# Expert weights through nine buffers and three split pieces, with regrouped gathers, in a two-layer hybrid block

## The chip, the cores and the metric

The kernel runs on one core of a Trainium2 chip. The metric is the device time of one execution in microseconds (us); lower is better. Engines are called PE (matmul; PEld is its weight load), DVE (vector), ACT (scalar), POOL (GpSimd) and SP (the engine whose queue issues the DMAs).

## The reference, cut to what matters

Two layers, each a token mixer and then a channel mixer. The second layer's channel mixer is the stage that the change touches: 256 tokens, width 1024, eight experts of hidden width 2816, two chosen for each token, everything in float32.

```python
def swiglu(x, w1, w3, w2):
    return (jax.nn.silu(x @ w1) * (x @ w3)) @ w2

def moe_swiglu(x, router, w1, w3, w2):
    logits = (x @ router).astype(jnp.float32)
    top_v, top_i = lax.top_k(logits, TOP_K)
    wts = jax.nn.softmax(top_v, axis=-1)
    gate = jnp.sum(jax.nn.one_hot(top_i, N_EXPERTS, dtype=jnp.float32) * wts[..., None], axis=-2)
    out = jnp.zeros(x.shape[:-1] + (w2.shape[-1],), x.dtype)
    for e in range(N_EXPERTS):
        out = out + gate[..., e:e + 1].astype(x.dtype) * swiglu(x, w1[e], w3[e], w2[e])
    return out
```

After it, `x = x + mod[5] * rms_norm(f, g_ffn_post[l])`: the residual x is needed again at the very end.

## The kernel before, in words

Everything up to the second layer's output projection is outside the change. At its end the router chooses experts, and `moe` starts. Each expert's three weight matrices (w1, w3, w2) are read once, each as 11 **chunks** of 1 MB (128 partitions by 2048 floats), so an expert is 33 chunks and the stage 264. A framework orders each engine's instructions ahead of time by priority and program order and adds the semaphores; a tile of a pool waits until the tile that held its slot before is released.

The experts run in the order q = 0 to 7 with the kinds `KINDS = "LSSLSSLS"`; which expert comes at which place is worked out on the device (`in_order`), so that the fuller ones come where room is larger. A **large** expert (`large`, room for 128 tokens) cuts each chunk into two **pieces** of 1024 columns. `split` (L366 to L368) rounds a piece on ACT into `hi`, and DVE subtracts it into `lo`; PE then multiplies hi by the tokens' hi, lo by hi, and hi by the tokens' lo: three matmuls where one would do at full precision of the operands (L1275 to L1277 for w1 and w3, L1366 to L1368 for w2). A chunk's buffer is free when DVE has made its second lo; a piece is free when PE has read it. A **small** expert (`small`, room for 64 tokens) multiplies the chunk itself, two column halves side by side (L1294, L1415); its buffer is free when PE has read it. Between the passes a large expert has `outer` (Silu on ACT, L1334) and `inner` (a product on DVE, four transposes on PE, a split, L1343 to L1349); the first two `inner` come before w2, four more within it.

`raw` (L1145) names the buffer of each chunk in the order of use: two tiles that are idle at the start (`sa0` and `kept`), then five `early` ones, each used once, and in between and ever after a ring. Before, that ring has six: three slots of the tag "raw" (the same that the earlier stages use) and three of the 13 slots of 8 KB a partition of the pool tag "S8". `piece_e` turns through five piece pairs: three of the tags "hi" and "lo", two more in S8. The 13 S8 slots in the experts' stage hold the normalized tokens (2), the ring (3), the tokens of large experts (`xes`, 2), the hidden values (`parts_u`, 3), the extra pieces (2) and the output sum (1). The trace calls S8 tiles "big".

`dispatch(qs, ...)` gathers the tokens of the experts qs with 32 matmuls (L1042) and scales them on ACT (L1204), and splits them for a large expert. `experts` runs it for `GROUPS[1:]` during the w3 pass of the experts `AT_GROUP`. The residual sits in an S8 tile until it is copied to `kept` (four ACT copies, L1439), and `kept` is itself the buffer of the second chunk.

SP's queue holds the weight loads in order; a load waits there for its buffer, and everything behind it waits too.

Of the kernel before, what the change touches and what calls it, by code (L numbers as in the profile page):

```python
# [10 lines left out]
R32 = mybir.dt.float32r  # L11
# [6 lines left out]
P = 128  # L18
D = 1024
KD = 8  # L20
# [8 lines left out]
N_AAC = 2  # L29
RATES = (0.661, 1.71, 1.045, 0.616, 1.995, 1.467, 0.55)  # L30
N_RAW = 3
N_RAW2, N_PC2 = 3, 2
N_PC = 3
N_EARLY = 5
LEAD = 3
# [11 lines left out]
AT_BACK, AT_NEXT = 2, 1  # L47
KINDS = "LSSLSSLS"
RANKS = (0, 1, 5, 2, 3, 6, 4)
GROUPS = ((0,), (1, 2, 3), (4, 5, 6), (7,))  # L50
AT_GROUP = (0, 2, 5)
ROOM = {"L": 128, "S": 64}
START = (0, 1, 2, 3, 'x', 'ctx')
# [3 lines left out]
def hybrid_kernel(ctx, tc, x, c, ctx_in, c_ctx, ada_w, ada_b, g_mix_pre, g_mix_post, g_ffn_pre, g_ffn_post,  # L57
# [4 lines left out]
    V, S, G, PE, SY = nc.vector, nc.scalar, nc.gpsimd, nc.tensor, nc.sync  # L62
# [12 lines left out]
    def nm(s):  # L75
        n_made[0] += 1
        return f"{s}{n_made[0]}"
# [7 lines left out]
    def sm(n, dt=F32):  # L85
        return st_.tile([P, n], dt, tag="sm", bufs=24, name=nm("sml"))
# [10 lines left out]
    def hot():  # L97
        return tc.high_priority(offset=PRI)
# [277 lines left out]
    def piece(shape):  # L376
        hi = st_.tile([P] + shape, R32, tag="hi", bufs=N_PC, name=nm("hi"))
        lo = st_.tile([P] + shape, R32, tag="lo", bufs=N_PC, name=nm("lo"))
        return hi, lo
# [686 lines left out]
    def moe(l, xt, route):  # L1066
# [12 lines left out]
        def weights():  # L1079
# [16 lines left out]
            PE.matmul(pr, ones, sel[:, 1], start=False, stop=True)  # L1096
            V.tensor_copy(cnt, pr)

        def in_order():

            key, rank = sm(NE), sm(N1)
            V.scalar_tensor_tensor(key, cnt, float(NE), ie, op0=OP.mult, op1=OP.add)
            square = lambda: s2([N1, N1])
            rows = lambda v: v.unsqueeze(1).to_broadcast([P, N1, N1])
            cols = lambda v: v.unsqueeze(2).to_broadcast([P, N1, N1])
            less, here = square(), square()
            V.tensor_tensor(less, rows(key[:, 1:]), cols(key[:, 1:]), op=OP.is_lt)
            V.tensor_reduce(rank, less, AX.X, OP.add)
            V.tensor_tensor(here, rows(rank), cols(rankq), op=OP.is_equal)
            yield  # L1110
            order, lens = sm(NE), sm(NE)
            todo = [(order, ie), (lens, cnt)] + [(to[:, t], of[:, t]) for to, of in ((slots, route.slot), (gates, gate)) for t in range(2)]
            for to, of in todo:
                picked = square()
                V.tensor_tensor(picked, here, rows(of[:, 1:]), op=OP.mult)
                V.tensor_reduce(to[:, 1:], picked, AX.X, OP.add)
                V.tensor_copy(to[:, 0:1], of[:, 0:1])
                yield
            V.tensor_copy(orderi, order)
            for q in range(NE):  # L1120
                if ROOM[KINDS[q]] < P:
                    V.tensor_scalar(lens[:, q:q + 1], lens[:, q:q + 1], float(P - ROOM[KINDS[q]]), None, op0=OP.add)
            V.reduce_max(most, lens, AX.X)
            V.tensor_copy(mosti, most)
# [13 lines left out]
                return self.tiles[(self.used - 1) % self.n]  # L1138
        sa0 = mo.tile([P, 1536 + 22 * 64], F32, name="sa")
        kept = mo.tile([P, 2 * D], F32, name="kept")  # L1140
        raws, xes, parts_u, pieces = Ring(N_RAW2, [2048]), Ring(2, [2, KD, P], R32), Ring(3, [2, 8, P], R32), Ring(N_PC2, [2, 1024], R32)
        ridx, early = [0], []
        inif = [False]

# [83 lines left out]
        def in_turn(*gens):  # L1228
            for g in gens:
                yield from g  # L1230
# [6 lines left out]
                        return  # L1237
                n = n and n - 1

        pidx = [0]  # L1240

        def piece_e():
            pidx[0] += 1
            if pidx[0] % (N_PC + N_PC2) < N_PC or inif[0]:
                return piece([1024])
            both = pieces()
            return both[:, 0], both[:, 1]

        def banks(ps, n, before):
            while len(ps) <= n:  # L1250
                if before:
# [3 lines left out]
        def flat_pass(wf, xe, aside=None, at=0, before=None):  # L1255

            ps = []
            for ch in range(11):
                if ch >= at:
                    run(aside, 1)  # L1260
                rw = raw(wf[:, ch * 2048:(ch + 1) * 2048])
                for hf in range(2):
                    with hot():
                        hi, lo = piece_e()
                        split(hi, lo, rw[:, hf * 1024:(hf + 1) * 1024])
                    f = ch * 2048 + hf * 1024
                    end = f + 1024
                    f_ = f
                    while f_ < end:
                        k, col = divmod(f_, FF)  # L1270
                        w = min(512 - col % 512, FF - col, end - f_)
                        banks(ps, col // 512, before)
                        o = ps[col // 512][:, col % 512:col % 512 + w]
                        hs, ls_ = hi[:, f_ - f:f_ - f + w], lo[:, f_ - f:f_ - f + w]
                        PE.matmul(o, xe[:, 0, k], hs, start=(k == 0), stop=False, skip_group_check=True)  # L1275
                        PE.matmul(o, xe[:, 0, k], ls_, start=False, stop=False, skip_group_check=True)
                        PE.matmul(o, xe[:, 1, k], hs, start=False, stop=(k == KD - 1), skip_group_check=True)  # L1277
                        f_ += w
            return ps
# [42 lines left out]
        def large(q, xe, behind, ahead):  # L1322

            pa = flat_pass(weight(moe_w1, q, "(p k) n -> p (k n)", k=KD), xe, behind, AT_BACK)
            run(behind)

            def cols(j):
                w = min(512, FF - 512 * j)
                return sa0[:, 512 * j:512 * j + w], w

            def outer(j):
                d, w = cols(j)
                with hot():
                    S.activation(d, pa[j][:, :w], AF.Silu)  # L1334
            yield
            pb = flat_pass(weight(moe_w3, q, "(p k) n -> p (k n)", k=KD), xe, ahead, AT_NEXT, outer)
            run(ahead)
            us = [parts_u() for _ in range(3)]

            def inner(j):  # L1340
                d, w = cols(j)
                with hot():
                    V.tensor_tensor(d, d, pb[j][:, :w], op=OP.mult)  # L1343
                    pt = tp()
                    dv = d.rearrange("s (a p r) -> s a r p", p=P, r=2)
                    for n in range(w // P):
                        PE.transpose(pt[:, n * P:(n + 1) * P], dv[:, n // 2, n % 2], ident)
                    o = slice(4 * j % 8, 4 * j % 8 + w // P)
                    split(us[j // 2][:, 0, o], us[j // 2][:, 1, o], pt[:, :w].rearrange("p (n s) -> p n s", s=P))  # L1349
            for j in range(U0):  # L1350
                inner(j)
            w2v = weight(moe_w2, q, "(a p r) n -> a p (r n)", p=P, r=2)
            py = [mm(), mx()]
            for a_ in range(11):
                rw = raw(w2v[a_])
                if a_ >= U1 and (a_ - U1) % 2 == 0 and U0 + (a_ - U1) // 2 < 6:
                    inner(U0 + (a_ - U1) // 2)
                for r in range(2):
                    with hot():
                        hi, lo = piece_e()  # L1360
                        split(hi, lo, rw[:, r * 1024:(r + 1) * 1024])
                    k = 2 * a_ + r
                    uh, ul = us[k // 8][:, 0, k % 8], us[k // 8][:, 1, k % 8]
                    for n in range(2):
                        cs = slice(n * 512, (n + 1) * 512)
                        PE.matmul(py[n], uh, hi[:, cs], start=(k == 0), stop=False)  # L1366
                        PE.matmul(py[n], uh, lo[:, cs], start=False, stop=False)
                        PE.matmul(py[n], ul, hi[:, cs], start=False, stop=(k == 21))  # L1368
            yield py
# [48 lines left out]
        def experts(base, fresh):  # L1418

            xs, backs, behind, group = [], [], None, []  # L1420
            before = dict(zip(AT_GROUP, GROUPS[1:])) if fresh else {q - 1: (q,) for q in range(1, NE)}
            if fresh:
                xs.append(xes())
                with tc.high_priority(offset=2 * PRI):
                    route.second_half(xs[0])
                weights()
                behind = in_order()
            else:
                run(dispatch((0,), base, xs))
            for q in range(NE):  # L1430
# [2 lines left out]
                    ahead.append(dispatch(before[q], base, xs))  # L1433
                do = (large if base or KINDS[q] == "L" else small)(q, xs.pop(0), behind, in_turn(*ahead))
                next(do)
                if fresh and q == 0:
                    for t in range(2):
                        for c in range(2):
                            S.copy(kept[:, 1024 * t + 512 * c:1024 * t + 512 * c + 512], xt[:, t, 512 * c:512 * c + 512])  # L1439
                if fresh and q == NE - 2:  # L1440
                    row = mo.tile([P, 2, 512], F32, name="row")
                    rows.extend([row[:, c] for c in range(2)])
# [9 lines left out]
                behind = None  # L1452
                if q % 2 or q == NE - 2:
                    behind = send_back(group, fresh and q == 1)
# [163 lines left out]
```

## Time and profile before

| | |
|---|---|
| median of 3 runs | 2069.02 us (2067.56 to 2077.01) |
| profiled execution | 2069.72 us, of which the span of the trace is 2068.0 us |
| PE busy | 1955.6 us (95% of the span) |
| DVE busy | 1306.7 us (63%) |
| ACT busy | 807.5 us (39%) |
| experts' stage | from about 1338 us to the end |
| DMA | 456.55 MB, mean 221 GB/s |

Busy time is a sum over the whole span and says little of one stage. The idle time of an engine is listed with what ended it. Matmuls overlap: a matmul of 512 columns is shown as 0.39 us long while the next starts 0.23 us after it, so distances between starts are the measure of PE's pace.

### The profile page before, as it was taken

Reading aid. Unit: us, or ns where it says so; the run is one execution under the profiler, and the core shown is the slowest. Engines: PE = TensorE matmul, PEld = TensorE weight load, DVE = VectorE, ACT = ScalarE, POOL = GpSimd, SP = SyncE. Lnnn points to the kernel's source line nnn. Section 1 sums busy time; section 2 is a strip of 40 time slices with the busy share of each in tenths; the row PEclk is TensorE's granted clock in tenths of the full one; section 3 lists DMA queues with packets and bytes.
Section 4 is the critical chain, followed back from the end, with each engine's and each line's share of the span. In section 5 each row is a group of like instructions: output and inputs, shape, how many; then the busy total and the mean of one; then the engine's idle time right before and its main releaser. Section 6 shows DMA issues by size and latency. Waiting matters only on the chain. (4 is left out here: it accounts for less than half of the span.)

```text
span 2068.0 us, 26249 instructions
## 1 busy us (share of the span) xinstructions
PE 1955.6 (95%) x9975; PEld 1423.8 (69%) x9975; DVE 1306.7 (63%) x2246; ACT 807.5 (39%) x1310; POOL 111.0 (5%) x183
## 2 busy tenths in 40 slices
PE   7999999989989999999999999999998999999996
PEld 3878777767878887887787889787332873437842
DVE  4896776689889869638976776787010870007812
ACT  3333334534352222226533475586020750006700
POOL 1000210030010000001002111000000000000000
PEclk9999999999999999999899999899999999999998
DMA  8324322335536567525333236569999989999996
GB/s 292 90 84 120 85 84 72 112 102 164 183 102 199 173 206 237 182 82 163 107 104 110 83 109 217 224 234 343 420 406 420 410 327 380 405 421 393 354 371 258
DMA packets 168197, 456.55 MB, mean 221 GB/s; under 512 B 11840, under 2 KB 84992, under 8 KB 134272
## 3 DMA queue, kind: packets, MB, share of 16 engines
q1 hardware_dynamic: 168064, 454.80, 60.3%
q8 instruction: 80, 1.31, 0.3%
q14 instruction: 53, 0.43, 0.1%
HBM read 450.05 MB, written 1.05 MB: 218 GB/s over the span
## 5 line engine op out<-in xcount | busy, mean ns | idle before, releaser
L385 PE MATMUL mm<-big,hi 128*128 128x512 f32 (+2 forms) x1328 | 481.4, 363 | 5.3 <-DVE mid L769 3.1
L386 PE MATMUL mm<-big,hi 128*128 128x512 f32 (+2 forms) x1328 | 476.3, 359 | 0.3 <-DVE sml L134 0.2
L387 PE MATMUL mm<-big,lo 128*128 128x512 f32 (+2 forms) x1328 | 475.7, 358 | 0.1
L367 ACT CAST hi<-raw 128x1024 fp32r<-128x1024 f32 (+1 forms) x276 | 286.3, 1046 | 471.1 <-PE mm L386 283.9
L368 DVE TENSOR_TENSOR lo<-raw,hi 128x1024 fp32r<-128x1024 f32 (+1 forms) x276 | 336.5, 1227 | 159.2 <-ACT hi L367 148.0
L385 PEld LDWEIGHTS mm<-big,hi 128*128 128x128 f32 (+1 forms) x1328 | 253.2, 191 | 56.6 <-issue 7.2
L386 PEld LDWEIGHTS mm<-big,hi 128*128 128x128 f32 (+1 forms) x1328 | 253.0, 191 | 42.6 <-issue 3.5
L387 PEld LDWEIGHTS mm<-big,lo 128*128 128x128 f32 (+1 forms) x1328 | 253.0, 190 | 40.1 <-issue 0.5
L276 DVE SCALAR_TENSOR_TENSOR aac<-raw,csil,aac 128x512 f32<-128x512 f32 x224 | 163.3, 765 | 2.9 <-DMA raw<-in_ada_w_dram 1.8
L1397 DVE TENSOR_TENSOR sa<-sa,mm 128x512 f32<-128x512 f32 x5 | 3.4, 689 | 218.7 <-PE mm L1294 218.7
L519 DVE SCALAR_TENSOR_TENSOR big<-ci,cdw,big 128x512 f32<-128x512 f32 (+1 forms) x240 | 132.9, 611 | 0.8
L1294 PE MATMUL mx<-big,mid 128*64 128x512 f32 (+1 forms) x358 | 99.3, 528 | 8.0 <-DMA big<-in_moe_w_dram 7.3
L1294 PE MATMUL mx<-raw,mid 128*64 128x512 f32 (+1 forms) x342 | 93.7, 518 | 6.4 <-DMA raw<-in_moe_w_dram 5.9
L1450 DVE SCALAR_TENSOR_TENSOR mid<-mm,sml,mid 128x512 fp32r<-128x512 f32 x8 | 6.0, 751 | 128.1 <-ACT mid L1449 128.1
L368 DVE TENSOR_TENSOR lo<-big,hi 128x1024 fp32r<-128x1024 f32 x61 | 72.9, 1221 | 9.2 <-ACT hi L367 8.4
L440 PE MATMUL mm<-hi,big 128*128 128x512 f32 x186 | 73.5, 395 | 0.0
L441 PE MATMUL mx<-lo,big 128*128 128x512 f32 x186 | 73.3, 394 | 0.0
L440 PE MATMUL mx<-hi,big 128*128 128x512 f32 x186 | 73.3, 394 | 0.0
L441 PE MATMUL mm<-lo,big 128*128 128x512 f32 x186 | 73.3, 394 | 0.0
L442 PE MATMUL mm<-hi,big 128*128 128x512 f32 x186 | 73.1, 393 | 0.0
L442 PE MATMUL mx<-hi,big 128*128 128x512 f32 x186 | 73.0, 393 | 0.0
L1294 PEld LDWEIGHTS mx<-big,mid 128*64 128x64 f32 x358 | 33.8, 140 | 53.9 <-issue 29.2
(414 smaller groups left out, 3310.4 us busy)
## 6 DMA issues: line engine op xcount, KB each, us to landing
big<-in_moe_w_dram SPq DMA_DIRECT2D x134, 1024.0 KB, 8.4
raw<-in_moe_w_dram SPq DMA_DIRECT2D x128, 1024.0 KB, 9.4
raw<-in_w_in_dram SPq DMA_DIRECT2D x56, 1024.0 KB, 5.3
raw<-in_ada_w_dram SPq DMA_DIRECT2D x41, 1024.0 KB, 5.1
raw<-in_ffn_w_dram SPq DMA_DIRECT2D x34, 1024.0 KB, 5.8
raw<-in_w_out_dram SPq DMA_DIRECT2D x8, 1024.0 KB, 5.1
big<-in_ada_w_dram SPq DMA_DIRECT2D x7, 1024.0 KB, 14.4
raw<-in_gla_proj_dram SPq DMA_DIRECT2D x4, 1024.0 KB
```

What stands on the lines that cost most here:

```text
L276: V.scalar_tensor_tensor(a, aw[:, k - 4 * r], col, a, op0=OP.mult, op1=OP.add)
L367: S.copy(hi, src)
L368: (eng or V).tensor_tensor(lo, src, hi, op=OP.subtract)
L385: PE.matmul(ps, hi[:, k, m0:m1], xh, start=(k == 0), stop=False)
L386: PE.matmul(ps, hi[:, k, m0:m1], xl, start=False, stop=False)
L387: PE.matmul(ps, lo[:, k, m0:m1], xh, start=False, stop=(k == kn - 1))
L440: PE.matmul(pss[t], a, hi[:, kk - k], start=(kk == 0), stop=False)
L441: PE.matmul(pss[t], a, lo[:, kk - k], start=False, stop=False)
L442: PE.matmul(pss[t], b, hi[:, kk - k], start=False, stop=(kk == kn - 1))
L519: V.scalar_tensor_tensor(acc, win, tap, acc, op0=OP.mult, op1=OP.add)
L1294: PE.matmul(ps[col // 1024][half:half + 64, col % 512:col % 512 + w], xe[:, k], rw[:, f_:f_ + w], start=(k == 0), stop=(k == KD - 1), skip ...
L1450: V.scalar_tensor_tensor(y[1], p_, back[1], y[0], op0=OP.mult, op1=OP.subtract)
```

## The change

The ring of chunk buffers grows from six to nine: `N_RAW2` is 6 instead of 3, so six S8 slots and the three "raw" slots. The extra pieces in S8 go (`piece_e` is removed; every piece is one of the three hi/lo pairs), and there is one `xes` tile instead of two. For that, the gathers are grouped otherwise: experts 1 and 2 during expert 0, then 3, 4, 5 during expert 2, then 6 and 7 during expert 5. The four copies of the residual to `kept` move from behind the w1 and w3 passes of expert 0 in the program into its w1 pass (`put_by`, two copies at each of two steps, ahead of `in_order`).

```diff
-N_RAW2, N_PC2 = 3, 2
+N_RAW2 = 6
...
-GROUPS = ((0,), (1, 2, 3), (4, 5, 6), (7,))
+GROUPS = ((0,), (1, 2), (3, 4, 5), (6, 7))
...
+        def put_by():
+
+            for t in range(2):
+                for c in range(2):
+                    S.copy(kept[:, 1024 * t + 512 * c:1024 * t + 512 * c + 512], xt[:, t, 512 * c:512 * c + 512])
+                yield
+
...
-        raws, xes, parts_u, pieces = Ring(N_RAW2, [2048]), Ring(2, [2, KD, P], R32), Ring(3, [2, 8, P], R32), Ring(N_PC2, [2, 1024], R32)
+        raws, xes, parts_u = Ring(N_RAW2, [2048]), Ring(1, [2, KD, P], R32), Ring(3, [2, 8, P], R32)
...
-        pidx = [0]
-
-        def piece_e():
-            pidx[0] += 1
-            if pidx[0] % (N_PC + N_PC2) < N_PC or inif[0]:
-                return piece([1024])
-            both = pieces()
-            return both[:, 0], both[:, 1]
-
...
-                        hi, lo = piece_e()
+                        hi, lo = piece([1024])
                         split(hi, lo, rw[:, hf * 1024:(hf + 1) * 1024])
...
-                        hi, lo = piece_e()
+                        hi, lo = piece([1024])
                         split(hi, lo, rw[:, r * 1024:(r + 1) * 1024])
...
-                behind = in_order()
+                behind = in_turn(put_by(), in_order())
...
-                if fresh and q == 0:
-                    for t in range(2):
-                        for c in range(2):
-                            S.copy(kept[:, 1024 * t + 512 * c:1024 * t + 512 * c + 512], xt[:, t, 512 * c:512 * c + 512])
```

## Rows read from the trace of the kernel before

**Rows 1.** The page: GB/s in 40 equal slices of the span.

```profile
GB/s 292 90 84 120 85 84 72 112 102 164 183 102 199 173 206 237 182 82 163 107 104 110 83 109 217 224 234 343 420 406 420 410 327 380 405 421 393 354 371 258
```

**Rows 2.** Windows: stretch, length, busy PE, PEld, DVE, ACT, POOL, clock, DMA share, GB/s.

```profile
1338.00:1460.00 122.00, 121.54 (x647) 96.28 (x649) 89.10 (x126) 83.54 (x116) 0.00 (x0) 0.98 0.76 287
1460.00:1600.00 140.00, 125.42 (x580) 47.11 (x577) 13.03 (x34) 16.26 (x46) 0.00 (x0) 1.00 1.01 415
1600.00:1720.00 120.00, 116.90 (x596) 89.88 (x595) 89.55 (x93) 73.77 (x83) 0.00 (x0) 1.00 0.91 359
1720.00:1866.00 146.00, 131.79 (x601) 51.08 (x601) 8.28 (x24) 10.09 (x26) 0.00 (x0) 0.96 1.00 415
1866.00:1986.00 120.00, 116.92 (x605) 90.71 (x602) 93.46 (x101) 74.09 (x85) 0.00 (x0) 1.00 0.92 359
```

**Rows 3.** Waits of SP's queue, 1600 to 1720 us: total, times, longest.

```profile
SPq L1157 <- DVE lo L368: 48.2, 19, 6.5
...
SPq L1157 <- PE mx L1294: 14.8, 4, 9.6
```

**Rows 4.** Timeline of SP's queue, 1240 to 1400 us: start, length, issues.

```profile
1299.29 9.49 SPq L1157 DMA_DIRECT2D raw<-in_moe_w_dram  x3
1318.03 33.15 SPq L1157 DMA_DIRECT2D big<-in_moe_w_dram  x9
1351.23 1.18 SPq L1157 DMA_DIRECT2D raw<-in_moe_w_dram  x2
1370.74 9.29 SPq L1157 DMA_DIRECT2D big<-in_moe_w_dram  x3
```

**Rows 5.** Timeline of PE in expert 3's w2 pass, a piece's first matmul and the next's.

```profile
1675.71 0.39 PE L1366 MATMUL mm<-hi,big 128*128 128x512 f32 x1
...
1677.08 0.39 PE L1366 MATMUL mm<-hi,big 128*128 128x512 f32 x1
```

**Rows 6.** Timelines of ACT and DVE in expert 3: splits back to back.

```profile
1685.89 2.00 ACT L367 CAST hi<-raw 128x1024 fp32r<-128x1024 f32 x2
...
1647.27 3.49 DVE L368 TENSOR_TENSOR lo<-raw,hi 128x1024 fp32r<-128x1024 f32 x3
```

**Rows 7.** Timelines in expert 0: a piece's last matmul and the cast it releases.

```profile
1342.81 0.40 PE L1277 MATMUL mm<-hi,big 128*128 128x512 f32 x1
...
1343.24 1.05 ACT L367 CAST hi<-raw 128x1024 fp32r<-128x1024 f32 x1 [1.16 <-PE mm L1277]
```

**Rows 8.** Timelines where expert 3 passes from w1 to w3: ACT, DVE, PE.

```profile
1630.75 0.60 ACT L1334 ACTIVATE sa<-mm 128x512 f32<-128x512 f32 x1 [2.44 <-PE mm L1277]
...
1634.09 1.23 DVE L368 TENSOR_TENSOR big<-raw,big 128x1024 fp32r<-128x1024 f32 x1 [4.52 <-ACT big L367]
...
1634.11 0.50 PE L1275 MATMUL mm<-big,big 128*128 128x512 f32 x1 [0.35 <-ACT big L367]
```

**Rows 9.** Timelines where expert 3 passes from w3 to w2: DVE, ACT, PE.

```profile
1662.98 0.69 DVE L1343 TENSOR_TENSOR sa<-sa,mm 128x512 f32<-128x512 f32 x1 [4.11 <-PE mm L1277]
...
1664.50 0.59 ACT L367 CAST big<-tp 128x512 fp32r<-128x512 f32 x1 [3.96 <-PE tp L1347]
...
1667.59 1.28 DVE L368 TENSOR_TENSOR big<-tp,big 128x512 fp32r<-128x512 f32 x2
...
1670.06 0.50 PE L1367 MATMUL mm<-lo,big 128*128 128x512 f32 x1 [0.52 <-DVE lo L368]
```

**Rows 10.** Timelines at expert 1: its first matmuls, and its first Silu.

```profile
1440.06 1.08 PE L1294 MATMUL mm<-raw,mid 128*64 128x512 f32 x4
...
1460.13 0.60 ACT L1386 ACTIVATE sa<-mm 128x512 f32<-128x512 f32 x1 [16.16 <-PE mm L1294]
```

**Rows 11.** Timeline of ACT: scaling gathered tokens; then the residual's copies and their waiter.

```profile
1365.95 1.12 ACT L1204 ACTIVATE mid<-tp,emod 128x128 f32<-128x128 f32 x3
...
L1439 ACT COPY kept<-big x4: 616/617/619, 1345.8 to 1349.3; 128x512 f32<-128x512 f32 x4
...
SPq L1157 <- ACT kept L1439: 14.8, 1, 14.8
```

## The prediction

> **What bounds the kernel now.** I read the page's slices first: moved bytes stay near 100 to 200 GB/s until the experts begin and then lie near 420 with dips [rows 1]. So the change lies in the one stage where the weight stream matters, and the question is what the dips are. I take 421 GB/s, the best slice, as the rate of the stream; a chunk of 1.0486 MB then needs 2.49 us, and 264 chunks need 657 us.
>
> The windows by stage show where the dips are [rows 2]. While small experts run, the stream is full (415 GB/s) and PE is partly idle: 125.4 of 140 us. There the DMA sets the pace. While the large ones run, PE is busy nearly throughout (116.9 of 120 us) and the stream falls to 359 GB/s, in expert 0 to 287. As lost stream time that is 120 x (1 - 359/421) = 17.7 us for expert 3, the same for expert 6, and 122 x (1 - 287/421) = 38.8 us for expert 0: 74 us in all. The small stretches lose 140 x (1 - 415/421) = 2.0, and 146 x (1 - 415/421) = 2.1 us.
>
> What the stream waits for is seen in SP's own queue [rows 3]: in expert 3 its loads stand for buffers, 48.2 us in 19 waits for a piece's lo (a chunk of a large expert used up) and 14.8 us in 4 waits for PE's reading of the next small expert's first chunk. All six buffers are full and PE is the slower side. A small expert is the reverse: its first pass of 11 chunks takes from 1440.1 to about 1460 [rows 10], so about 1.85 us a chunk, against 2.49 from the DMA. The kernel therefore alternates between a producer that is faster and one that is slower than its consumer, and each buffer that is full when a large expert ends is stream time saved.
>
> The order at the start shows the same ring [rows 4]: by 1352 the queue has issued 16 of expert 0's chunks (14 in these rows, and the two into the tiles idle at the start), then it stands until 1370.7, when the ring slot for chunk 17 comes free.
>
> **The ring, six to nine.** A large expert takes a fixed time on PE. During it the stream moves 33 chunks and fills the ring for what follows: six chunks before, nine after. If the large expert lasts as long as before, each of the three gives 3 x 2.49 = 7.5 us of idle stream back, 22.4 us together. The idle time is there to give (17.7, 17.7 and 38.8). In expert 0 it works from the start: the three "raw" slots and the S8 slots together let 19 chunks be issued where 16 are now, before the same stand at about 1371.
>
> Is the lead lost again? Nine chunks are 22.4 us of stream; a small expert regains (2.49 - 1.85) x 33 = 21 us. After experts 0 and 3 two small ones follow, so it is regained wholly. After expert 6 there is one, and 21 of 22.4 us is nearly enough: 1 us may stay behind. In the small stretches a deeper ring also covers moments when PE is late (gathers, returns): 4 us are lost there now; I count 1 us net of the above, with bounds 0 and 4.
>
> **Three piece pairs instead of five.** This is the cost, and it lies in the same three stages. In steady state: a piece of w2 occupies PE 1677.08 - 1675.71 = 1.37 us [rows 5]. ACT's casts follow each other at 2.00 - 1.05 = 0.95 us, DVE's subtractions at (3.49 - 1.22)/2 = 1.14 us [rows 6]; neither bounds. But with three pairs the cast of piece n waits for PE's last matmul of piece n - 3. From that matmul's start to the cast there are 0.43 us [rows 7]; then 1.05 for the cast, 0.1 of handing over, 1.22 for lo, 0.1 again: lo is there after 2.9 us. PE needs it after the rest of that matmul (0.23), two more pieces (2.74) and one matmul with hi alone (0.23): 3.2 us. The loop fits with 0.3 us to spare. With five pairs 3.0 us are to spare.
>
> So every interruption of ACT or DVE beyond 0.3 us now reaches PE. Three kinds occur in each large expert:
> - From w1 to w3, Silu stands in ACT's order between casts. DVE was without work for 4.5 us there, and PE lost 0.35 us at the first wait because it had five pieces in stock [rows 8]. With two fewer in stock, 2.74 us of cover are gone; but the casts are also made later, nearer to PE, so less of them stands behind the Silu. I take 1.2 us; bounds 0 and 2.7.
> - From w3 to w2, DVE waits 4.1 us for PE, then makes two products (0.69 each) and two extra splits (1.28 for the pair), 2.6 us of other work; PE lost 0.5 us [rows 9]. With the smaller stock I take 1 us more; bounds 0 and 2.7.
> - Four more `inner` within w2: 0.69 on DVE, 0.59 on ACT, about 0.65 on DVE, at three moments. Each beyond 0.3 us gives 0.35 + 0.3 + 0.35 = 1.0 us, but PE has the four transposes of about 0.4 us to do meanwhile and the stock was small here before. I take 0.3 each, 1.2 in all; bounds 0 and 4.
>
> With small ones (returns, one-hot rows) that is 3.5 us a large expert, 10.5 us over three; bounds 0 and about 10 an expert. It counts fully, because in a large expert the stream stands and a longer one only lengthens that.
>
> **Gathers regrouped.** Expert 0 loses one large expert's share: four steps with two scalings of 0.37 us (1.12/3) [rows 11], a small cast and its subtraction, and 32 gather matmuls of half the width: about 4 us less on ACT, 2 on DVE, 1.5 on PE, in a stage where PE is full. I take 2 us gained; bounds 0 and 4. The same work goes to expert 5, a small one, where DVE and ACT are busy 8 and 10 of 146 us [rows 2]: nothing, as long as its gather ends before expert 6, with the whole w2 pass between. One `xes` tile is enough since each large expert's tokens are then gathered after the previous large one has ended.
>
> **The residual's copies.** Four copies of 0.62 us, already run at 1345.8 to 1349.3; one load waited 14.8 us for the slot [rows 11]. The second chunk leaves `kept` only when its lo is made, so at most 3 us earlier; and the load concerned is long before the stand at 1371. On ACT the pair (1.2 us) now falls between casts with 0.3 us to spare: I take 1 us lost; bounds 0 and 2. Pushing `in_order` two steps back delays the expert order to about 1360; the first load that needs it comes when expert 1's chunks are due, after 1410: nothing.
>
> **Sum.** 22.4 + 1 + 2 - 10.5 - 1 = 13.9 us gained. On the profiled execution's 2069.7 us that is 2055.8; the median of the runs shown is 0.7 us lower, so 2055.
>
> **A page against it.** The rows give the stream 415 to 421 GB/s while small experts run [rows 1, 2]. The Trainium skill, "DMA: Bandwidth & Descriptors", section Specifications, gives about 358 GB/s as a core's HBM limit. By that page a chunk takes 2.93 us (an estimate), large experts would run at the DMA's pace, and the sum would be about 2069. The trace disagrees: its small experts are some 60 GB/s above the page's limit.
>
> **The rivals.**
> - *The pieces eat the gain.* If the transitions and `inner` cost 6 to 8 us a large expert, inside the bounds above, the sum is 22.4 + 2 - 18 to 24: 0 to 6 us gained, some 2066. For it: DVE and ACT are busy 90 and 74 of 120 us in expert 3, so little slack remains to refill a stock. Against it: within w2 the stock was already small and PE hardly waited. Chance 0.20.
> - *Slower.* The loop of three pairs takes longer than PE's three pieces in steady state (for instance an order on ACT or DVE that puts other work into it each time). It breaks even at 24.4/198 = 0.12 us a piece (three experts of 66 pieces) and is slower by 0.5% at 0.18. At 0.2 us, 39.6 us lost, it gives 2069.7 - 24.4 + 39.6 = 2085. Only 0.3 us a loop (0.1 a piece) separates the loop from PE's pace. Against it: the chain above, read link by link, fits. Chance 0.11.
> - *The stream is bound anyway.* If the 359 GB/s of the large experts [rows 2] were all that the DMA can give beside a busy PE, more buffers would give nothing, and the piece cost would hide behind the stream: 2069. The waits for buffers [rows 3] speak against it. Chance 0.01. The page just named would make this the case.
> - *The slots come late.* The first chunks now all need S8 slots, which come free from 1318 on [rows 4], where two "raw" ones were used from 1299; should a hot load take the slot that the router's tile needs, experts begin some 9 us later: 2064. Chance 0.02.
>
> **How the numbers follow.** Forecast 0.66, the rivals 0.20, 0.11, 0.01, 0.02. I give the time of the forecast, 2055; its own range, with the piece cost between 1 and 6 us an expert, is 2047 to 2062. The range for 8 in 10 reaches from 2043 (piece cost near nothing, all bounds of gains) to 2069 (pieces eat everything). About 10 us, 0.5%, is what a measurement of this kernel tells from no change. Faster by more than that (below 2058.7) is the forecast but for 0.05 at its upper end: 0.61; within it are that end and the first, third and fourth rival: 0.28; slower is the second: 0.11.
>
> **What would show it.** Right: windows like [rows 2] with 359 GB/s risen to about 380 in experts 3 and 6; 19 chunks issued before the stand at 1371; SP's wait for PE at the end of a large expert no longer the longest; PE waits for hi and lo at the two transitions, one to two us each; small experts at 415 GB/s and above until the end. Wrong: large experts that last over 107 us instead of about 100 (pieces), PE waits at every piece (loop), a later first expert matmul than 1338 (slots), or a last expert whose PE has no idle time (lead not regained).

## The result, and the profile after

The changed kernel takes 2047.98 us (median of 4 runs, 2043.80 to 2052.43) against 2068.29 us (2067.35 to 2077.01) of the kernel before on the same chip: ratio 0.9894, 95% interval 0.9863 to 0.9926, which is 20.3 us less. The forecast was 2055, so 14 us less, with a range of 2043 to 2069. The profiled execution after took 2049.26 us, with a span of 2047.5.

The slices of the page again come first (GB/s in 40 equal slices of the changed kernel's span), and then its windows by stage, cut at the same places of the work as [rows 2] with the last expert added (columns as there).

```profile
GB/s 296 88 86 111 79 96 69 124 83 166 185 98 190 177 193 244 208 87 139 145 85 120 97 83 185 263 185 348 389 420 420 420 417 350 419 420 420 380 373 257
```

```profile
1340.00:1462.00 122.00, 120.22 (x625) 95.50 (x626) 90.67 (x121) 82.97 (x104) 0.00 (x0) 0.96 0.74 282
1462.00:1595.00 133.00, 124.93 (x600) 51.73 (x598) 13.02 (x34) 16.23 (x46) 0.00 (x0) 1.00 1.01 420
1595.00:1715.00 120.00, 116.91 (x599) 89.40 (x595) 90.51 (x93) 76.24 (x83) 0.00 (x0) 1.00 0.96 390
1715.00:1852.00 137.00, 125.39 (x602) 51.32 (x601) 10.37 (x30) 13.88 (x38) 0.00 (x0) 1.00 1.01 420
1852.00:1972.00 120.00, 116.92 (x598) 90.76 (x595) 95.13 (x101) 77.15 (x85) 0.00 (x0) 0.99 0.96 383
1972.00:2022.00 50.00, 49.01 (x238) 20.95 (x234) 3.07 (x7) 3.11 (x8) 0.00 (x0) 1.00 1.01 420
```

Against [rows 1, 2]: of the slices from the first 420 to the last but one, five lay below 400 before (327, 380, 393, 354, 371) and three do now (350, 380, 373); experts 3 and 6 move 390 and 383 GB/s where they moved 359, the small stretches 420 where they moved 415. PE's busy time in expert 3 is the same to 0.01 us (116.91 of 120). The stretches of small experts have become shorter, 140 to 133 us and 146 to 137.

Where the time went is clearest from PE's own marks: from the first matmul of w1 to the last of w2 for each large expert, and the gaps between them for the small ones. Each number below is the distance of two rows in PE's timeline of one profiled execution, in us; "stage" runs from expert 0's first matmul to the end of the last small expert's w2.

| kernel | expert 0 | 1, 2 | expert 3 | 4, 5 | expert 6 | 7 | stage | first matmul at |
|---|---|---|---|---|---|---|---|---|
| before | 101.7 | 163.1 | 98.9 | 169.4 | 98.9 | 79.5 | 711.6 | 1338.0 |
| after | 105.2 | 152.9 | 99.1 | 160.5 | 99.9 | 71.2 | 688.8 | 1340.7 |

The small experts are 27.4 us shorter (10.2, 8.9, 8.3), the large ones 4.7 us longer, 3.5 of it in expert 0, and the stage begins 2.7 us later: 20.0 us net. The gain is earned in a large expert, by filling buffers, and shows in the small one behind it, which finds its weights there.

SP's queue in expert 3 of the changed kernel (waits from 1600 to 1720 us: total, times, longest), the answer to [rows 3]:

```profile
SPq L1164 <- DVE lo L368: 71.3, 30, 3.6
SPq L1164 <- PE mx L1292: 13.2, 5, 6.9
```

The queue stands longer than before (71.3 us for lo where it was 48.2), and yet the stream is fuller. A standing queue is not an idle stream: what was issued is still landing meanwhile. So the total of these waits is no measure of the loss; the GB/s of the same stretch shows it.

And the start (timelines of SP's queue in three windows, and below them its waits from 1300 to 1400 us), the answer to [rows 4, 11]:

```profile
1301.45 9.48 SPq L1164 DMA_DIRECT2D raw<-in_moe_w_dram  x3
...
1313.90 14.51 SPq L1164 DMA_DIRECT2D big<-in_moe_w_dram  x9
...
1347.21 0.33 SPq L1164 DMA_DIRECT2D big<-in_moe_w_dram  x1
...
1364.85 1.91 SPq L1164 DMA_DIRECT2D big<-in_moe_w_dram  x4
```

```profile
SPq L1164 <- DVE lo L368: 50.0, 9, 17.2
...
SPq L1164 <- ACT kept L1103: 9.4, 1, 9.4
```

Two chunks in the idle tiles and these 3 + 9 + 1 make 15 that are issued before the queue stands from 1347.5 to 1364.9. The prediction had 19 before a stand at 1371. It missed that the first ten S8 chunks, with the normalized tokens (2) and the tokens of expert 0 (1), already fill the 13 S8 slots: the tenth takes the one that the residual gave back. The wait for the residual's copy has shrunk from 14.8 to 9.4 us.

### The profile page after: what moved, and what is told of

Same layout as the page of the kernel before. It is cut to its first block, busy times and chain, and to the rows that moved or that the text cites. A ratio compares the mean times of both kernels' runs of the same rounds, so it can differ in the third digit from the quotient of the medians.

```text
span 2047.5 us, 26265 instructions
## 1 busy us (share of the span) xinstructions
PE 1948.6 (95%) x9975; PEld 1431.4 (70%) x9975; DVE 1312.0 (64%) x2246; ACT 816.8 (40%) x1310; POOL 109.4 (5%) x183
## 5 line engine op out<-in xcount | busy, mean ns | idle before, releaser
L368 DVE TENSOR_TENSOR lo<-big,hi 128x1024 fp32r<-128x1024 f32 x142 | 170.6, 1222 | 31.6 <-ACT hi L367 28.4
L367 ACT CAST hi<-big 128x1024 fp32r<-128x1024 f32 x142 | 148.2, 1052 | 47.0 <-PE mx L1275 23.4
L1292 PE MATMUL mx<-big,mid 128*64 128x512 f32 (+1 forms) x446 | 120.2, 512 | 3.2 <-DMA big<-in_moe_w_dram 2.9
L1292 PE MATMUL mm<-big,mid 128*64 128x512 f32 (+1 forms) x240 | 83.9, 548 | 2.0 <-DMA big<-in_moe_w_dram 1.9
L1292 PEld LDWEIGHTS mx<-big,mid 128*64 128x64 f32 x446 | 43.7, 136 | 52.3 <-issue 38.5
L1274 PE MATMUL mx<-lo,big 128*128 128x256 f32 (+1 forms) x228 | 76.9, 340 | 0.1
L1275 PE MATMUL mx<-hi,big 128*128 128x256 f32 (+1 forms) x228 | 75.4, 336 | 0.0
L440 PE MATMUL mm<-hi,big 128*128 128x512 f32 x186 | 73.6, 396 | 0.0
L440 PE MATMUL mx<-hi,big 128*128 128x512 f32 x186 | 73.4, 395 | 0.0
L1413 PE MATMUL mm<-big,sa 128*64 128x512 f32 x288 | 69.9, 598 | 3.7 <-DMA big<-in_moe_w_dram 2.4
```

The costliest lines, as they stand in the source:

```text
L367: S.copy(hi, src)
L368: (eng or V).tensor_tensor(lo, src, hi, op=OP.subtract)
L440: PE.matmul(pss[t], a, hi[:, kk - k], start=(kk == 0), stop=False)
L1292: PE.matmul(ps[col // 1024][half:half + 64, col % 512:col % 512 + w], xe[:, k], rw[:, f_:f_ + w], start=(k == 0), stop=(k == KD - 1), skip ...
L1413: PE.matmul(py[64 * n:64 * n + 64], u[:, k], rw[:, c:c + 512], start=(k == 0), stop=(k == 21))
```

## The experiments

All ratios are to the kernel before, run on the same chip in turn; the figure in us takes the ratio times 2069. Differences of two ratios carry the root of the sum of squares of their half-widths. The theory on test: deeper ring good, about 7.5 us a buffer; piece pairs bad, 3.5 us a large expert; gathers and copies small. The rivals: the pieces cost nothing or much more, and the rest of the change has effects of its own.

**The ring alone, at six and seven buffers.** All of the change but the number of buffers (`ring7` has 4 here).

```diff
-N_RAW2 = 6
+N_RAW2 = 3
```

> The changed kernel with the ring of chunk buffers back at six (three S8 slots stay empty), three piece pairs. If the ring is the source of the gain, each large expert ends with three chunks fewer in stock: 3 x 7.5 = 22 us and the dips in the small experts come back, so 2070 to 2075 us, with about 355 GB/s in expert 3. If the gain came from the regrouped gathers, the early copies or the earlier first loads, it stays below 2056.

> The changed kernel with a ring of seven and three piece pairs. If every buffer is worth one chunk for each of three large experts (7.5 us), 2048 + 15 = 2063 us, 7 us below the ring of six. If the gain needs the whole nine (the stand in expert 0 only), it stays at the ring of six's time.

Six buffers: 2077.20 us, 1.0037 (1.0015 to 1.0059). Seven: 2068.95 us, 0.9975 (0.9956 to 0.9994). The changed kernel itself, run again on another chip:

> The changed kernel once more, on the chip that runs the others of this call. 2048 us within its spread (2044 to 2052).

It gave 2053.48 against 2074.08 us, 0.9889 (0.9873 to 0.9906).

| kernel | expert 0 | 1, 2 | expert 3 | 4, 5 | expert 6 | 7 | stage | first matmul at |
|---|---|---|---|---|---|---|---|---|
| six buffers | 103.6 | 163.5 | 99.0 | 167.6 | 101.5 | 79.4 | 714.6 | 1340.8 |
| seven | 104.3 | 158.0 | 99.0 | 167.8 | 101.1 | 76.4 | 706.7 | 1340.2 |
| nine, again | 105.3 | 153.6 | 99.0 | 160.5 | 101.2 | 71.8 | 691.4 | 1343.6 |

From six to nine the stage falls by 714.6 - 690.1 = 24.5 us (690.1 is the mean of the two profiled executions with nine), 8.2 a buffer; by the ratios it is 0.0148, 31 us with about 6 either way. The forecast was 23.4. The 24.5 is rather low: in the executions with nine the mean clock is 0.98 in expert 0 and 0.98 to 0.99 in expert 6, with six it is 1.00 in both, which is some 3 us (an estimate). Without the three buffers the rest of the change costs 7.7 us (3.1 to 12.2), where the forecast had 9.5 (10.5 + 1 - 2); by the stage, 714.6 against 711.6, it is 3.0.

Windows of about 20 us through expert 3 show when the stream is idle: six buffers first, then the changed kernel (columns as in [rows 2]).

```profile
1624.00:1644.00 20.00, 19.41 (x104) 15.85 (x103) 15.50 (x14) 16.56 (x20) 0.00 (x0) 1.00 1.01 415
1644.00:1664.00 20.00, 20.00 (x120) 17.53 (x119) 17.08 (x16) 14.71 (x15) 0.00 (x0) 1.00 0.99 384
1664.00:1684.00 20.00, 19.36 (x97) 15.51 (x96) 18.20 (x20) 14.34 (x16) 0.00 (x0) 1.00 0.88 328
1684.00:1706.00 22.00, 22.00 (x99) 17.41 (x98) 18.91 (x19) 14.73 (x16) 0.00 (x0) 1.00 0.93 332
1706.00:1724.00 18.00, 18.00 (x86) 8.22 (x85) 4.98 (x11) 1.64 (x3) 0.00 (x0) 1.00 0.75 264
```

```profile
1635.00:1655.00 20.00, 20.00 (x119) 17.50 (x119) 17.04 (x16) 14.63 (x15) 0.00 (x0) 1.00 1.01 420
1655.00:1675.00 20.00, 19.36 (x97) 15.51 (x96) 18.16 (x20) 14.36 (x16) 0.00 (x0) 1.00 1.01 419
1675.00:1698.00 23.00, 23.00 (x103) 18.12 (x101) 18.88 (x19) 14.88 (x17) 0.00 (x0) 1.00 0.96 379
1698.00:1715.00 17.00, 17.00 (x82) 7.50 (x81) 4.98 (x11) 1.47 (x3) 0.00 (x0) 1.00 0.71 262
```

With six the stream begins to fall back some 36 us into the expert (1644 against a first matmul at 1607.9): lost time 20 x (1 - 384/421) = 1.8, then 4.4, 4.6 and 6.7, with 0.3 for the 415, 17.8 us in all. With nine it is full for 76 us (1598.8 to 1675) and loses 2.3 + 6.4 = 8.7. The difference, 9.1 us, is what the three buffers give in this expert; the forecast had 7.5. What stays is mostly the passage to the small expert (from 1698), which no buffer here has touched (6.7 us with six, 6.4 with nine).

**The pieces alone, with seven buffers** (S8 has room for both only there): five pairs again.

```diff
-N_RAW2 = 4
+N_RAW2, N_PC2 = 4, 2
...
-                        hi, lo = piece([1024])
+                        hi, lo = piece_e()
```

> The same ring of seven, with five piece pairs again (two in S8), so only the piece count differs from the run with seven. If three pairs cost what the prediction took, 3.5 us a large expert, this is 10 us faster than that run, about 2053. If the loop of three pairs is hidden in large experts (durations of 99 us in expert 3 in both kernels' traces), the two agree within 3 us.

2065.88 us, 0.9970 (0.9951 to 0.9990), against 0.9975 with three pairs: 1 us, with 6 either way, where 10.5 was forecast. Expert 3 is the place to see it. First and last matmul of that expert in PE's timelines, three pairs and then five:

```profile
1602.58 0.48 PE L1273 MATMUL mm<-hi,big 128*128 128x512 f32 x1
...
1701.57 0.40 PE L1366 MATMUL mx<-hi,big 128*128 128x512 f32 x1
```

```profile
1600.64 0.47 PE L1282 MATMUL mm<-hi,big 128*128 128x512 f32 x1
...
1699.65 0.40 PE L1375 MATMUL mx<-hi,big 128*128 128x512 f32 x1
```

98.99 and 99.01 us: two more pairs give this expert nothing. Expert 0 is another matter. By the same marks the kernel with five pairs has

| kernel | expert 0 | 1, 2 | expert 3 | 4, 5 | expert 6 | 7 | stage | first matmul at |
|---|---|---|---|---|---|---|---|---|
| seven, five pairs | 102.5 | 158.9 | 99.0 | 168.9 | 100.9 | 77.3 | 707.5 | 1339.2 |

so its expert 0 is 1.9 us shorter than with three pairs (104.3), expert 6 by 0.2, and the small experts take it back. The 1.9 us arise where expert 0 passes from w1 to w3: 40 matmuls, from 36.7 us into the expert on, take 9.1 us with three pairs and 7.2 with five. There ACT has, besides six Silus, a load of its function table between its casts. Expert 3 has the six Silus alone at its passage, so the load is the likely cause; no run shows it by itself. ACT's timeline with three pairs, then PE's waits from 1376 to 1386 us (with five pairs, from 1374 to 1386, there is none):

```profile
1376.21 1.28 ACT L1332 ACT_TABLE_LOAD   x1
```

```profile
PE mx L1273 <- ACT hi L367: 0.5, 1, 0.5
PE mm L1274 <- DVE lo L368: 0.3, 1, 0.3
```

The two waits are 0.8 of the 1.9 us; the rest is in distances between matmuls too small to be listed as waits.

**Two pairs, to see the loop.** The changed kernel with two pairs used in turn.

```diff
+            if len(pairs) < 2:
+                pairs.append(piece([1024]))
+            pidx[0] += 1
+            return pairs[(pidx[0] - 1) % 2]
...
-                        hi, lo = piece([1024])
+                        hi, lo = piece_e()
```

> The changed kernel with two piece pairs in the experts instead of three. By the loop worked out in the prediction (lo is there 2.9 us after the last matmul of the piece before last; PE needs it after 0.23 + 1.37 + 0.23 = 1.83) every piece waits 0.5 us: 66 pieces x 0.5 = 35 us a large expert, 134 instead of 99 us, and about 2048 + 90 to 105 = 2138 to 2153 us. If the loop has more room than that (PE starts many hi matmuls ahead of the first lo), less than half of it, below 2100.

2115.49 us, 1.0211 (1.0180 to 1.0243). Large experts last 131.0, 123.8 and 124.6 us, some 25 us more, which is 25/66 = 0.38 us a piece, less than the 0.5 that were expected and more than half of it. ACT's timeline and PE's in expert 3 of this kernel:

```profile
1718.41 1.05 ACT L367 CAST hi<-raw 128x1024 fp32r<-128x1024 f32 x1 [2.06 <-PE mx L1376]
```

```profile
1720.78 0.51 PE L1375 MATMUL mm<-lo,big 128*128 128x512 f32 x1 [0.54 <-DVE lo L368]
```

ACT waits for PE's last matmul of a pair, PE then for the lo made from it: the loop that the prediction worked out link by link. It does not fit with two pairs; with three it does, but for the passage in expert 0.

**The residual's copies late again.** In the program the copies stand behind both passes of expert 0, as before; `run` gives them raised priority, which the kernel before did not.

```diff
-                behind = in_turn(put_by(), in_order())
+                behind = in_order()
...
+                if fresh and q == 0:
+                    run(put_by())
```

> The changed kernel with the residual's copies back behind the two passes in the program. If their place matters little, within 3 us of the changed kernel. If the earlier release of the residual's slot carries part of the gain (one more chunk ahead of the stand in expert 0), 2.5 us or more slower. By the prediction's term, 1 us faster.

2053.09 us, 0.9888 (0.9867 to 0.9910), against 0.9889 of the changed kernel on the same chip. But this does not test the copies, since they did not move: in both traces ACT and DVE run the same instructions in the same order, the last copy starts 5.8 us after the first expert matmul (1351.5 against 1345.7 here, 1349.4 against 1343.6 in the changed kernel), and one load waits 9.4 us for them. In the kernel before the last copy started 11.3 us after that matmul (1349.3 against 1338.0).

**The gathers alone, in the kernel before.**

```diff
-GROUPS = ((0,), (1, 2, 3), (4, 5, 6), (7,))
+GROUPS = ((0,), (1, 2), (3, 4, 5), (6, 7))
```

> The kernel before with the gathers regrouped and nothing else. If a shorter expert 0 gives time, 2 us faster (2066) and an expert 0 of about 99 to 100 us instead of 102. If PE, not the gathers, sets expert 0, no difference.

2081.14 us, 1.0027 (1.0014 to 1.0040): 5.6 us slower (2.9 to 8.3), where 2 us faster was forecast. In its profiled execution expert 0 takes 104.8 us (before: 101.7), experts 3 and 6 take 100.5 (98.9). The 1.5 us more in expert 3 arise at its start. The 3 us before its first matmul, and the 3 us from it on, partly at the lower clock:

```profile
1604.70:1607.70 3.00, 1.14 (x11) 0.69 (x7) 1.74 (x4) 2.46 (x3) 0.00 (x0) 1.00 1.01 421
1607.70:1610.70 3.00, 3.00 (x11) 2.40 (x11) 3.00 (x5) 2.45 (x5) 0.00 (x0) 0.66 1.02 423
```

In expert 0 the gather itself takes part. Here it runs in parts of 16, 8 and 8 matmuls between 1364.0 and 1371.2 us, and the clock from 1368 to 1372 is 0.71. In the changed kernel it is one block. PE's timeline in that kernel's expert 0, then ACT's, then two windows of the same place:

```profile
1351.46 1.98 PE L1042 MATMUL tp<-mid,big 128*128 128x128 f32 x16
1353.93 2.93 PE L1042 MATMUL tp<-mid,big 128*128 128x128 f32 x16 [0.49 <-ACT mid L1211]
1356.66 0.73 PE L1274 MATMUL mm<-lo,big 128*128 128x512 f32 x1
```

```profile
1352.58 3.78 ACT L1211 ACTIVATE mid<-tp,emod 128x64 f32<-128x64 f32 x12 [0.48 <-PE tp L1042]
```

```profile
1352.00:1356.00 4.00, 3.44 (x26) 3.16 (x26) 1.81 (x2) 3.50 (x13) 0.00 (x0) 0.92 0.00 0
1356.00:1360.00 4.00, 4.00 (x15) 3.36 (x15) 1.06 (x1) 2.67 (x7) 0.00 (x0) 0.65 0.00 0
```

All 32 gather matmuls stand in one block, the twelve scalings keep ACT from casting for 3.8 us, PE waits 0.49 us for the scalings, and the granted clock is 0.65 in the 4 us that follow: a matmul that takes 0.39 us at full clock is shown with 0.63 there. In the kernel before, pieces stood between the parts of the gather, and its granted clock was 1.00 from 1358 to 1370 and from 1385 to 1389 us, where it ran.

**The same gather spread out.** In the changed kernel, expert 0's gather at ordinary priority, so that the pieces go first:

```diff
-                with hot():
+                with (ExitStack() if calm[0] else hot()):
...
+            calm[0] = q == 0 and not inif[0]
```

> The changed kernel with expert 0's gather for experts 1 and 2 at ordinary instead of raised priority, so that its matmuls stand between those of the w3 pass. In the changed kernel the 32 gather matmuls run in two blocks at 1351 to 1357 us, PE waits for ACT between them and the granted clock falls to 0.65 in that stretch. If that block is the regrouping's price, expert 0 takes 102 instead of 105 us and the kernel 3 us less, ratio about 0.9875. If the price lies elsewhere, no difference (0.989).

2050.02 us, 0.9888 (0.9866 to 0.9911). Its expert 0 takes 102.2 us, the 3 us won back, and its clock there is full:

```profile
1354.00:1358.00 4.00, 4.00 (x25) 3.55 (x25) 3.25 (x4) 3.11 (x4) 0.00 (x0) 1.00 0.00 0
...
1593.50:1596.50 3.00, 1.14 (x11) 0.69 (x7) 1.75 (x4) 2.47 (x3) 0.00 (x0) 1.00 0.99 412
1596.50:1599.50 3.00, 3.00 (x11) 2.37 (x11) 2.86 (x4) 1.64 (x4) 0.00 (x0) 0.68 1.03 426
```

But the time is that of the changed kernel, 0.9889: its expert 3 begins at a clock of 0.68 and takes 100.6 us, and experts 1 and 2 take 153.7. Of the 3 us in expert 0, the clock is about 1.7 (0.08 x 4 + 0.35 x 4 of the windows above) and the rest is PE standing idle, 1.3 us within expert 0 against 0.1 with the gather spread out. The ring of ten below bears this out: it has the same block at full clock, and PE idle as much,

```profile
1348.00:1352.00 4.00, 3.43 (x24) 3.00 (x24) 0.80 (x1) 3.99 (x14) 0.00 (x0) 1.00 0.00 0
```

and its expert 0 takes 103.3 us, 102.1 with the gather spread out.

**The old groups with nine buffers.** The tokens of large experts and the hidden values share four S8 tiles in a fixed turn, which makes room for the old order.

```diff
-GROUPS = ((0,), (1, 2), (3, 4, 5), (6, 7))
+GROUPS = ((0,), (1, 2, 3), (4, 5, 6), (7,))
...
+        turns = {False: [0, 1, 2, 3, 0, 2, 3, 0, 1, 3, 0, 1], True: [0, 1, 2, 3]}
+        parts_u = xes
```

> The changed kernel (ring of nine, three piece pairs, early copies) with the gathers grouped as before; the second large token tile that this needs is one of the three tiles of the hidden values, which are free at those times (in the branch for more than 128 tokens, which these inputs do not take, each expert's tokens are gathered before it). If the regrouping costs what the kernel with the regrouping alone showed (1.0027, 5.6 us), this is some 5 us faster than the changed kernel: ratio about 0.9865, expert 0 about 102 us. If that loss belonged to the small ring only, the same as the changed kernel, 0.989.

2048.21 us, 0.9882 (0.9857 to 0.9907). Expert 0 takes 102.6 us, expert 3 99.0; the total is again within its uncertainty of the changed kernel. So at nine buffers the price of the regrouping is too small to be told here, though expert 0 alone is shorter by 2.6 us.

**Ten buffers.** The tokens of large experts share the three tiles of the hidden values, and the slot that comes free goes to the ring.

```diff
-N_RAW2 = 6
+N_RAW2 = 7
...
-        raws, xes, parts_u = Ring(N_RAW2, [2048]), Ring(1, [2, KD, P], R32), Ring(3, [2, 8, P], R32)
+        raws, parts_u = Ring(N_RAW2, [2048]), Ring(3, [2, 8, P], R32)
+        xes = parts_u
```

> The changed kernel with a ring of ten: the large experts' tokens take one of the three tiles of the hidden values, which are not in use at the same time, and the slot goes to the ring (in the branch for more than 128 tokens, which these inputs do not take, each expert's tokens are gathered before it). If every buffer is worth 2.5 us a large expert and the last small expert can still use the lead, 7 us faster than the changed kernel, 2041; since that expert can regain about 21 us and ten chunks are 25, rather 5 us, 2043. If the lead of nine is all that the small experts can take, no difference.

> The ring of ten with the same ordinary priority for expert 0's gather. If both gains add, 3 us below the ring of ten: ratio about 0.982. If not, 0.9836.

Ten: 2040.76 us, 0.9836 (0.9820 to 0.9853), faster than both kernels. Ten with the gather spread out: 2042.14 us, 0.9850 (0.9827 to 0.9873), no further gain. Against nine on the same chip the tenth buffer is worth 0.0053, 11 us with 5 either way, by the ratios; in the profiled executions the stage falls from 690.1 to 684.7 us, 5.4 (its expert 3 takes 100.6 us, with the clock fallen at its start). End of expert 3 and passage to expert 4 with ten:

```profile
1663.00:1688.00 25.00, 25.00 (x113) 19.93 (x113) 22.45 (x24) 18.31 (x21) 0.00 (x0) 1.00 1.00 403
1688.00:1705.00 17.00, 17.00 (x78) 8.64 (x79) 6.92 (x13) 2.47 (x4) 0.00 (x0) 1.00 0.72 252
```

Lost are 1.1 + 6.8 = 7.9 us, against 8.7 with nine. The end of the large expert is now nearly full; the passage is as it was. There SP's queue waits 6.9 us at once for PE's reading of the small expert's chunk, in both kernels, and the tenth buffer did not change that.

## Why the prediction was right, and where it was not

- **What bounds the stage: right.** The stream was idle in the large experts for want of buffers, and each buffer gives back stream time there. Six, seven, nine and ten buffers make stages of 714.6, 706.7, 690.1 and 684.7 us: 7.9, 8.3 and 5.4 a buffer where 7.5 was worked out. The rival of a bound stream is out: from 1635 to 1675 us the stream moves 420 and 419 GB/s beside a PE that is busy for 39.4 of 40 us. What the prediction had not located is when in the expert the stream stands: in its second half and at the passage.
- **The three pairs: the term that was mis-sized.** 10.5 us were charged; with seven buffers the three experts show 2.1 (1.9, 0.0 and 0.2), and the whole kernel 1 us with 6 either way. The step that was mis-sized is that of the interruptions with their smaller stock. Of the passages (1.2 and 1 us an expert) only one cost what was charged, or more: the first, in expert 0, 1.9 us. In expert 3 neither the passages nor the `inner` within w2 (1.2 us) cost anything that can be seen. PE's waits for pieces in the whole stage of the changed kernel (total, times, longest):

```profile
PE mm L1365 <- DVE lo L368: 1.0, 2, 0.5
PE mx L1273 <- ACT hi L367: 0.9, 3, 0.5
...
PE mm L1273 <- ACT hi L367: 0.7, 2, 0.4
...
PE mm L1273 <- ACT big L367: 0.5, 1, 0.5
PE mm L1274 <- DVE lo L368: 0.3, 1, 0.3
```

  That is 3.4 us over three large experts; the like rows of the kernel before add up to 3.0 (waits as they are listed; the smallest are not). Why it is so little in expert 3 is seen in ACT's order from w1 to w3, the answer to [rows 8]:

```profile
1625.98 1.05 ACT L367 CAST hi<-big 128x1024 fp32r<-128x1024 f32 x1 [0.69 <-PE mx L1275]
1626.93 0.59 ACT L1332 ACTIVATE sa<-mm 128x512 f32<-128x512 f32 x1
1628.08 1.09 ACT L1332 ACTIVATE sa<-mx 128x512 f32<-128x512 f32 x2 [0.56 <-PE mx L1275]
```

  With five pairs ACT had cast as far ahead as it could and then stood 2.44 us for PE before its first Silu [rows 8]. With three it arrives there just in time: the Silu follows a cast without a gap. The shorter stock took from ACT's waiting, not from PE's work. The prediction had named this ("the casts are also made later") and counted it too low. In steady state its loop was right: ACT now waits again and again for PE to release a piece, 49 times at one line and 44 at another, and expert 3 is no longer for it; at two pairs it is. ACT's waits in the changed kernel's stage:

```profile
ACT hi L367 <- PE mx L1275: 31.2, 49, 3.7
...
ACT hi L367 <- PE mx L1366: 17.7, 44, 1.2
```

- **The regrouped gathers: wrong sign.** The prediction counted 4 us less work on ACT and called it 2 us gained. Alone it costs 5.6 us (2.9 to 8.3); its profiled execution is 3.1 us longer in expert 0 and 1.5 and 1.6 in experts 3 and 6, which begin at a fallen clock. For expert 0 of the changed kernel the cause is shown: the gather forms one block, PE waits, and the clock falls. What the regrouping has to do with the clock of experts 3 and 6 is not shown. With the ring at nine the price is not to be told from zero (0.9882 with the old groups, 0.9888 spread out, 0.9889 and 0.9894 as changed), though both variants shorten expert 0 by some 3 us. In their profiled executions later stretches are longer by parts of that; which part is due to the gathers stays open.
- **The copies: not tested.** One us was charged, and the run that was to move them back left them where they were. What shows is that they end earlier than was thought possible, by some 5.5 us against expert 0's first matmul where at most 3 was forecast, and that the load's wait for them is 5.4 us shorter.
- **The sum.** Ring 23.4 forecast, 24.5 by the stages and 31 with 6 either way by the ratios; the rest 9.5 forecast, 7.7 (3.1 to 12.2) measured, 3.0 by the stages. The size of the rest was near by chance: pieces too dear by 8 to 10, gathers too cheap by about 8. The time came out 7 us below the forecast.
- **The signs promised.** Right: experts 3 and 6 at about 380 GB/s (390, 383), small experts above 415 to the end (420), no large expert over 107 us. Wrong: 19 chunks before the first stand (15; the next load waits for a lo, so for the slot of an earlier chunk, since all 13 S8 slots were in use); PE waits of one to two us at each passage (3.4 us listed in all, and 1.9 us more with three pairs than with five at one passage of expert 0); SP's wait for PE at the end of a large expert no longer the longest (6.9 us, shorter than 9.6 but still the longest). The later first matmul (1340.7 against 1338.0) was a sign for late slots; but like programs begin between 1335.2 and 1345.7, so it says nothing. And the last expert is now nearly all PE (49.0 of 50 us), which was the sign of a lead not wholly regained; its stretch is still 8.3 us shorter.
- **Open.** The stage with six buffers (714.6 us) is 3.7 us shorter than in the kernel before with the new groups alone (718.3). Fewer pairs need not be the quicker: the mean clock of the kernel with the groups alone is 0.98 in each of its large experts (1346 to 1445, 1607 to 1708, 1878 to 1979 us), with six buffers 1.00 in each (1345 to 1445, 1607 to 1707, 1874 to 1976), which is some 2 us an expert and more than the whole difference. Why the clock falls in the one and not in the other stays open, and one profiled execution of each is all that this rests on.

## What to carry to other kernels

Where a kernel alternates between stretches in which its consumer is slower and faster than the stream, price a buffer by the stream's idle time in the slow stretches, in short windows, and not by the total of the queue's waits: here it gave about 8 us a MB until the large experts ran full, and the next loss then lay at the passage between two kinds. Stock between engines cost little to give up as long as the loop through the remaining pieces was shorter than the consumer's pace; work it out link by link, as three pairs fit and two cost 25 us an expert. What was left to pay came where another engine had much else to do at once, 1.9 us at one passage of expert 0. Work that is moved or shrunk is to be priced by where its instructions then stand in each engine's order, since in expert 0 a smaller gather in one block cost more than a larger one spread out (105.2 against 102.6 us). And an edit of the program's text need not move anything in the engines' order, which is to be read before its time counts: the one for the copies moved nothing.

## What the runs showed of the hardware

PE's granted clock fell where large experts begin in some executions and not in others, with the same activity ahead of it. In the 3 us before expert 3's first matmul PE is busy for 1.14 us in the changed kernel, in the one with the gather spread out and in the one with the new groups alone. The first then stays at full clock (2.4 GHz); the clock of the next 3 us is 0.68 and 0.66 in the others (shown above), a mean of time at that level and at 1.2 GHz. The changed kernel:

```profile
1595.80:1598.80 3.00, 1.14 (x11) 0.68 (x7) 1.74 (x4) 2.46 (x3) 0.00 (x0) 1.00 1.01 418
1598.80:1601.80 3.00, 3.00 (x15) 2.47 (x15) 2.87 (x4) 2.36 (x4) 0.00 (x0) 1.00 1.01 418
```

Nor does one order of work settle it: the kernel with the copies late, whose ACT and DVE orders are those of the changed kernel, has the gather's block at full clock (1.00 from 1354 to 1366 us), and its expert 0 takes 103.6 us where the changed kernel's takes 105.2 and 105.3. Each such fall is worth about 1.5 us of a large expert (99.0 without, 100.5 with), as much as several of the terms that were worked out, so differences of a us or two between single profiled executions are to be held against the clock first.

And the stream kept 420 GB/s through 133 us, on the one core that runs here. The Trainium skill, "DMA: Bandwidth & Descriptors", section Specifications, lists about 358 GB/s as the HBM limit of a core; the same page's section Bandwidth gives that figure as a core's share when both cores of an HBM domain stream, so it was no bound for this kernel, and the prediction read it as one.
